# Modulation weights in two halves with longer rows, the first two u weight tiles in one transfer, and x transposed by a diagonal

## The chip, the cores and the metric

The kernel runs on one core of one Trainium2 chip. The metric is device microseconds of one execution; the figure of a version is the median of its runs.

In this text PE is TensorE (the matmul engine), PEld its weight loads, DVE VectorE, ACT ScalarE, POOL GpSimd and SP the engine that issues most transfers. Every engine works through its own queue in order; a transfer that SP can't issue yet holds up all that are queued behind it on SP.

## What is computed

One layer of a streaming encoder, over 1024 prompt rows and 32 sample rows of width 1024. What matters here is its beginning:

```python
mod = silu(c) @ w_mod + b_mod                     # c: one row for the prompt, one for the samples
shift, scale, gate = split(mod, 3)                # 1024 columns each
h = x / sqrt(mean(x*x) + eps) * g_norm            # each row of x
h = h * (1 + scale) + shift
z = h @ w_in                                      # 5704 columns, the first 512 are u
u, zs, q, k, v, ... = split(z)
```

Behind it come the state space model on u, an indexed sparse attention, gates, an output projection and a last normalization; they are the same before and after the change.

## The kernel before, in words

`h` is wanted with its columns on the partitions (`hH` and `hL`, the high and low parts of each value), since it is the moving operand of every projection. The 1056 rows are cut into three blocks of 256, 384 and 416 columns of `h` (`BW`), made of 2, 3 and 4 row tiles (`ROWS`; the last tile holds the 32 sample rows). The 1024 columns of x are eight column tiles, k = 0 to 7.

The opening goes through these steps; the two letters are those of the list `START` (lines 48 to 59), which fixes the order of the work on all engines by hand. Its tokens are read from left to right (lines 771 to 782) and each engine gets its instructions in that order.

- `sq`, `ss`, `sc` (lines 211 to 223): ScalarE sums the squares of a row tile, DVE and POOL make the row's reciprocal root `rstd`, and DVE multiplies the whole 128 x 1024 tile by it, in place.
- `ld` (line 739): SP issues loads. `ld21` of the modulation weights loads column group 2, half 1; `ldx67` loads row tiles 6 and 7; `ldz` the next projection weights and the SSM's loads. What stands ahead of the list (lines 749 to 759) is issued at once.
- `mm`, `row`, `co`, `ap` (lines 284 to 304): modulation in four column groups j of 256 columns, each with scale columns (h = 0) and shift columns (h = 1). One group and half is a tile of 8 x 256 columns from a transfer with rows of 1 KB (line 282). TensorE makes eight f32 products with 32 columns of weights, four side by side in the array; ScalarE copies the result to SBUF; two products with a selection matrix (`sel2`) turn it so that it lies on the partitions; three small DVE steps give `scl` and `sh` for column tiles 2j and 2j+1.
- `xt` (line 227): TensorE transposes column tile k of all row tiles of a block into PSUM, by an identity. There are two such PSUM buffers.
- `hf`, `sp` (lines 233 and 241): ScalarE applies `scl` and `sh`; DVE splits the result into `hH` and `hL`.
- `wl` (line 729): the u weights of a group of 128 columns are split into high and low parts; group 0 by ScalarE and DVE, group 1 on POOL. They are loaded in two transfers with rows of 512 bytes (lines 726 and 250).
- `ub` (line 543): three products (lines 271 to 273) add column tile k of a block to u of group 0 or 1.
- `a` with a number: so many of the small DVE steps of the SSM's constants.

Tiles of the tag `wm` share five buffers (`WB`): modulation weights, and row tiles 6 to 8 of x. A load into a reused buffer waits on SP until the last reader is through.

After the list, line 526 turns the SSM's C matrices by transposes (line 529), and the projections for the rest of z run through `Stream`, interleaved with the SSM and the attention by fixed costs.

Of the kernel before, what the change touches and what calls it, by code (L numbers as in the profile page):

```python
# [7 lines left out]
F32 = mybir.dt.float32  # L8
# [4 lines left out]
ALU = mybir.AluOpType  # L13
# [3 lines left out]
T, TS, D = 1024, 32, 1024  # L17
# [4 lines left out]
KT = 8  # L22
# [8 lines left out]
WB = 5  # L31
# [14 lines left out]
MR, ML, YS, YW, HI, HG, JO, SF = (), 1, 10, 15, 0, 0, 8, (2, 2, 2, 1)  # L46
C_U, C_ZS, C_Q, C_K, C_V, C_ZA, C_QI, C_KI, C_GM = 0, 512, 1024, 1536, 2048, 2560, 3072, 3584, 3656
START = """
    sq0 ss0 sq1 sc0 ss1 sq2 sc1 ss2 sc2 mm00 srow ldw21 a13 xt00 row00 xt01 co00 mm01 ldw30 row01 wl00 co01
    ap0 mm10 ldw31 a2 hf00 row10 xt02 sp00 hf01 co10 sp01 xt03 mm11 ldx67 a6 wl10 ub000 row11 co11 sq3 ub100  # L50
    ap1 ub001 a1 ub101 hf02 ss3 a1 hf03 sp02 sq4 sp03 ub002 ub102 sq5 ss4 ub003 sc3 ub103 sc4 mm20 ldx8 ldz
    ss5 row20 a2 co20 sc5 a5 mm21 xt10 row21 xt11 hf10 co21 hf11 ap2 xt12 sp10 xt13 hf12 mm30 hf13 xt04 sp11
    row30 ub010 hf04 co30 sp12 xt05 xt14 hf05 ub110 sp13 hf14 mm31 sp04 xt15 row31 xt06 hf15 ub011 sp05 co31
    sq6 xt07 ap3 ub111 ub012 sp14 hf06 ub112 hf07 xt16 sp15 ub013 sq7 xt17 sp06 ub113 up hf16 ub004 sp07
    ub104 hf17 ub014 sp16 sq8 ub114 sp17 ub005 zs ub105 ss6 ub015 ss7 ss8 ub115 ub006 ub106 sc6 ub016 ub116
    sc7 ub007 sc8 ub107 ue00 ub017 ue10 a5 xt20 ue01 xt21 ub117 hf20 ue11 sp20 hf21 xt22 a1 ub020 hf22 xt23
    sp21 ub120 hf23 xt24 sp22 ub021 ub121 hf24 sp23 xt25 ub022 hf25 sp24 xt26 ub122 hf26 ub023 sp25 xt27
    ub123 sp26 hf27 ub024 ub124 sp27 ub025 ub125 ub026 ub126 ub027 ub127 ue02 ue12
    """
# [1 line left out]
GROW = [[n for g_, _, n in ROWS if g_ == g] for g in range(3)]  # L61


def body(nc, tc, I, O, dbg=None):
# [3 lines left out]
    te, ve, se, ge, sp = nc.tensor, nc.vector, nc.scalar, nc.gpsimd, nc.sync  # L68
# [48 lines left out]
    idf = cst.tile([128, 128], F32, name="idf")  # L117
# [6 lines left out]
    w_in = I["w_in"].rearrange("o d e -> (o d) e")  # L124
    w_mod = I["w_mod"].rearrange("o d e -> (o d) e")
# [31 lines left out]
    sc2 = cst.tile([128, 2, 8], F32)  # L157
# [3 lines left out]
    scP = cst.tile([128, 8, 32], F32, name="scP")  # L161
# [7 lines left out]
    bmod = pcol[:, 8:32]  # L169
# [5 lines left out]
    srow = pp.tile([80, 128], F32)  # L175
# [12 lines left out]
    scl = cst.tile([128, 8, 2], F32)  # L188
# [7 lines left out]
    def xload(i):  # L196
        g, r, n = ROWS[i]
        if i < 2:
            xt = stg.tile([128, D], F32, name="xt", tag="stg")
        elif i < 5:  # L200
            xt = XH[i // 4][:, D * (i == 3):D * (i == 3) + D]
        elif i == 5:
            xt = pa.tile([128, D], F32, name="xt", bufs=1)
        else:
            if i % 2 == 0:
                XW.append(pa.tile([128, 2, D], F32, name="xw", tag="wm", bufs=WB))
            xt = XW[-1][:, i % 2]
# [10 lines left out]
        ve.tensor_scalar(ss[:n, i:i + 1], ss[:n, i:i + 1], 1.0 / D, EPS, op0=ALU.mult, op1=ALU.add)  # L218
        ge.tensor_tensor(rstd[:n, i:i + 1], ss[:n, i:i + 1], nhalf[:n, i:i + 1], op=ALU.pow)

    def xscale(i):
        g, r, n = ROWS[i]
        ve.tensor_scalar_mul(XG[g][r][:n], XG[g][r][:n], rstd[:n, i:i + 1])

    PX, HX = {}, {}

    def xtrans(g, k):
        px = ps_z("px")
        PX[g, k] = px
        for r, n in enumerate(GROW[g]):  # L230
            te.transpose(px[:, r * 128:r * 128 + n], XG[g][r][:n, k * 128:(k + 1) * 128], idf[:n, :n])
# [16 lines left out]
    def wload(src, kt, n, pool=None):  # L248
        raw = (pool or wst).tile([128, kt, n], F32, tag="raw", name="raw", bufs=2)
        sp.dma_start(raw, src.rearrange("(k p) e -> p k e", p=128))  # L250
        return raw
# [21 lines left out]
        te.matmul(ps, wl, xh, start=False, stop=last)  # L273
# [5 lines left out]
    def mod_load(j, h):
        wm = WM[j, h] = pa.tile([128, 8, 256], F32, name="wm", tag="wm", bufs=WB)  # L280
        c = (1024, 0)[h] + 256 * j
        sp.dma_start(wm, w_mod[:, c:c + 256].rearrange("(k p) e -> p k e", p=128))

    def mod_mm(j, h):
        for k in range(8):
            te.matmul(pmrow[32 * (k % 4):32 * (k % 4) + 32, 256 * h:256 * h + 256], scP[:, k], WM[j, h][:, k],
                      start=k < 4, stop=k >= 4)

    def mod_row(j, h):
        MR_[j, h] = pa.tile([128, 256], F32, name="mrow", bufs=2)  # L290
        se.copy(MR_[j, h], pmrow[:, 256 * h:256 * h + 256])

    def mod_cols(j, h):
        for i in range(2):
            ch = (8, 0)[h] + 2 * j + i
            te.matmul(pmod[:, 2 * ch:2 * ch + 2], MR_[j, h][:, 128 * i:128 * i + 128], sel2, start=True, stop=True)

    def mod_apply(j):
        kk = slice(2 * j, 2 * j + 2)
        ks = slice(8 + 2 * j, 10 + 2 * j)  # L300
        bc2 = lambda ap: ap.unsqueeze(2).to_broadcast([128, 2, 2])
        ve.tensor_tensor(scl[:, kk], pm[:, ks], bc2(bmod[:, ks]), op=ALU.add)
        ve.tensor_tensor(scl[:, kk], scl[:, kk], bc2(gcol[:, kk]), op=ALU.mult)
        ve.tensor_tensor(sh[:, kk], pm[:, kk], bc2(bmod[:, kk]), op=ALU.add)
# [166 lines left out]
    for k in range(7):  # L471
        n = 1 << k
# [250 lines left out]
    ord_.enter_context(tc.manual_schedule())  # L723
    raw = {}

    def uload(q):
        raw[q] = wload(w_in[:, C_U + 128 * q:C_U + 128 * q + 128], KT, 128)

    def uparts(q):
        UW[q] = wparts(raw[q], KT, 128, leng=ve) if q == 0 else wparts(raw[q], KT, 128, pool=pa, heng=ge, bufs=1)  # L730
# [20 lines left out]
    mod_load(0, 0)
    mod_load(0, 1)
    uload(0)
    mod_load(1, 0)
    mod_load(1, 1)
    uload(1)
    for i in range(3, 6):
        xload(i)
    mod_load(2, 0)
    ve.tensor_add(sel2, idf[:, 0:2], idf[:, 32:34])  # L760
    for j in (64, 96):
        ve.tensor_add(sel2, sel2, idf[:, j:j + 2])
# [1186 lines left out]
```

## Time and profile before

| | us |
|---|---|
| median of three runs | 1014.81 |
| lowest and highest of them | 1013.17, 1015.25 |
| the profiled execution | 1013.51 |
| its span, first to last instruction | 1011.5 |
| first u product starts | 24.70 |
| last u product of the list starts | 70.37 |
| first transpose after the list starts | 70.56 |

| engine, busy over the span | us | share |
|---|---|---|
| PE | 968.2 | 96% |
| DVE | 763.3 | 75% |
| ACT | 524.6 | 52% |
| POOL | 234.6 | 23% |

How to read it. A row of the timeline has the start, the time of the merged instructions, the engine and line, the operation, its output and inputs, their shapes and how many instructions stand in it; in brackets the idle time before it and what ended that. Matmuls are pipelined, so that the time of one overlaps the next, and what one costs is seen from start to start. A row of the stages has, for each engine, the busy time and the number of instructions, then the TensorE clock that was granted (1.00 is full speed), the busy share of the 16 DMA engines and GB/s.

### The profile page before, as it was taken

Reading aid. Unit: us, or ns where it says so; the run is one execution under the profiler, and the core shown is the slowest. Engines: PE = TensorE matmul, PEld = TensorE weight load, DVE = VectorE, ACT = ScalarE, POOL = GpSimd, SP = SyncE. Lnnn points to the kernel's source line nnn. Section 1 sums busy time; section 2 is a strip of 40 time slices with the busy share of each in tenths; the row PEclk is TensorE's granted clock in tenths of the full one; section 3 lists DMA queues with packets and bytes.
Section 4 is the critical chain, followed back from the end, with each engine's and each line's share of the span. In section 5 each row is a group of like instructions: output and inputs, shape, how many; then the busy total and the mean of one; then the engine's idle time right before and its main releaser. Section 6 shows DMA issues by size and latency. Waiting matters only on the chain.

```text
span 1011.5 us, 16910 instructions
## 1 busy us (share of the span) xinstructions
PE 968.2 (96%) x6034; PEld 904.1 (89%) x6034; DVE 763.3 (75%) x1747; ACT 524.6 (52%) x1126; POOL 234.6 (23%) x443
## 2 busy tenths in 40 slices
PE   5999999999999999999999989999998999999997
PEld 2789999999998898999999979899897989898786
DVE  4669979994776878889999976577577785885543
ACT  3642234433555656858896365565575564443111
POOL 3202400000000024343322743233222222430000
PEclk9999999999999999999999999999999999999999
DMA  9923425437484222333323422231329403552311
GB/s 315 289 66 101 133 70 140 113 95 203 164 256 151 64 63 64 105 83 98 118 74 114 141 87 64 85 106 55 107 66 332 136 22 109 182 188 105 126 63 62
DMA packets 134400, 124.24 MB, mean 123 GB/s; under 512 B 20401, under 2 KB 115077, under 8 KB 134317
## 3 DMA queue, kind: packets, MB, share of 16 engines
q1 hardware_dynamic: 133376, 122.62, 39.3%
q8 instruction: 47, 0.77, 0.3%
q10 hardware_dynamic: 780, 0.52, 0.2%
q14 instruction: 37, 0.30, 0.1%
q0 software_dynamic: 160, 0.03, 0.0%
HBM read 87.74 MB, written 34.83 MB: 121 GB/s over the span
## 4 chain that ended last, share of the span: by engine, by line
PE 50%; DVE 14%; ACT 10%; issue 4%; DMA 1%; POOL 0%; SPq 0%; POOLq 0%; ACTq 0%; DVEq 0%
PE pz L271 8%; PE pz L272 7%; PE pz L273 7%; ACT junkb L1567 7%; PE pss L1403 3%; PE pt L1496 3%; DVE junk L1569 3%; PE psm L1918 3%; PE psm L1919 3%; PE psm L1920 3%; PE pspo L1515 2%; PE pspo L1513 2%; PE psm L272 1%; PE psm L273 1%; PE psm L271 1%
## 5 line engine op out<-in xcount | busy, mean ns | idle before, releaser
L271 PE MATMUL pz<-hH,wh 128*128 128x384 f32 (+4 forms) x744 | 254.5, 342 | 2.4 <-ACT tg L713 2.0
L272 PE MATMUL pz<-hL,wh 128*128 128x384 f32 (+4 forms) x744 | 246.2, 331 | 0.0
L273 PE MATMUL pz<-hH,wl 128*128 128x384 f32 (+4 forms) x744 | 246.0, 331 | 0.0
L264 POOL TENSOR_TENSOR wl<-raw,wh 128x256 fp32r<-128x256 f32 (+1 forms) x180 | 134.7, 776 | 126.5 <-ACT wh L259 116.0
L271 PEld LDWEIGHTS pz<-hH,wh 128*128 128x128 f32 (+1 forms) x744 | 140.4, 189 | 7.5 <-ACT tg L713 2.3
L272 PEld LDWEIGHTS pz<-hL,wh 128*128 128x128 f32 (+1 forms) x744 | 139.9, 188 | 1.8
L273 PEld LDWEIGHTS pz<-hH,wl 128*128 128x128 f32 (+1 forms) x744 | 139.6, 188 | 1.4
L1567 ACT ACTIVATE junkb<-sco,thr 128x768 bf16<-128x768 f32 (+3 forms) x128 | 96.7, 756 | 31.0 <-DVE thr L1643 20.1
L1569 DVE TENSOR_SCALAR_CACHE_REDUCE junk<-sco,thr 128x1024 bf16<-128x1024 f32 (+2 forms) x96 | 105.5, 1098 | 2.2
L271 PE MATMUL pss<-hH,wh 128*128 128x256 f32 (+2 forms) x304 | 97.6, 321 | 0.1
L272 PE MATMUL pss<-hL,wh 128*128 128x256 f32 (+2 forms) x304 | 95.7, 315 | 0.0
L273 PE MATMUL pss<-hH,wl 128*128 128x256 f32 (+2 forms) x304 | 95.4, 314 | 0.0
L263 POOL CAST wh<-raw 128x256 fp32r<-128x256 f32 x88 | 38.0, 471 | 180.9 <-PE pz L272 109.6
L1498 ACT CAST PH<-pt 128x512 fp32r<-128x512 f32 (+2 forms) x96 | 43.0, 482 | 41.5 <-PE pt L1496 37.4
L1499 DVE TENSOR_TENSOR PL<-pt,PH 128x512 fp32r<-128x512 f32 (+2 forms) x96 | 50.4, 551 | 14.6 <-ACT PH L1498 13.7
L271 PEld LDWEIGHTS pss<-hH,wh 128*128 128x128 f32 x304 | 58.6, 193 | 2.6 <-issue 1.6
L272 PEld LDWEIGHTS pss<-hL,wh 128*128 128x128 f32 x304 | 58.1, 191 | 0.3 <-DVE hL L78 0.2
L1236 DVE SCALAR_TENSOR_TENSOR sco<-rl,wi,sco 128x384 f32<-128x384 f32 (+6 forms) x49 | 46.9, 963 | 15.2 <-ACT rl L1231 14.1
L273 PEld LDWEIGHTS pss<-hH,wl 128*128 128x128 f32 x304 | 58.1, 191 | 0.0
L1231 ACT ACTIVATE rl<-pss 128x384 f32<-128x384 f32 (+6 forms) x56 | 40.9, 738 | 28.6 <-PE pss L1229 23.1
L1416 ACT ACTIVATE Sm<-Sm,mx 128x128 f32<-128x128 f32 (+8 forms) x68 | 52.7, 775 | 0.8 <-DVE mx L1409 0.8
L1920 PE MATMUL psm<-o,mL 128*128 128x512 f32 (+1 forms) x136 | 51.8, 381 | 0.0
(401 smaller groups left out, 2174.9 us busy)
## 6 DMA issues: line engine op xcount, KB each, us to landing
raw<-in_w_in SPq DMA_DIRECT2D x44, 512.0 KB
thD<-tg SPq DMA_DIRECT2D x16, 528.0 KB
wm<-in_w_mod SPq DMA_DIRECT2D x8, 1024.0 KB
tgl<-thD SPq DMA_DIRECT2D x8, 528.0 KB
m<-thD SPq DMA_DIRECT2D x8, 528.0 KB
rraw<-in_w_mod SPq DMA_DIRECT2D x4, 1024.0 KB
kd<-kd SPq DMA_DIRECT2D x32, 128.0 KB
xo<-in_x_prompt SPq DMA_DIRECT2D x8, 512.0 KB
```

Source lines behind the costliest of these rows:

```text
L264: leng.tensor_sub(wl[:, c], raw[:, c], f32(wh[:, c]))
L271: te.matmul(ps, wh, xh, start=first, stop=False)
L272: te.matmul(ps, wh, xl, start=False, stop=False)
L273: te.matmul(ps, wl, xh, start=False, stop=last)
L1231: se.activation(rl[:m, :nk].rearrange("p (b c) -> p b c", c=w_), pv, AF.Relu)
L1236: ve.scalar_tensor_tensor(sco[i][:m, :nk], rl[:m, :nk], w, sco[i][:m, :nk], op0=ALU.mult, op1=ALU.add)
L1416: se.activation(P, P, AF.Exp, scale=-1.0, bias=self.mx, accum_out=self.rs)
L1498: se.copy(PH[:, b0:b1_, oc], src)
L1499: ve.tensor_sub(PL[:, b0:b1_, oc], src, f32(PH[:, b0:b1_, oc]))
L1567: se.activation(junkb[:m, :nk], x[:m], AF.Sign, bias=t, accum_out=cnt[:m, k:k + 1])
L1569: ve.tensor_scalar(junk[:m, :nk], x[:m], t, None, op0=ALU.is_lt, op1=ALU.add, accum_out=cnt[:m, k:k + 1])
L1920: te.matmul(ps, ml, wh, start=False, stop=last)
```

## The change

- Modulation is computed in two halves of 512 scale and 512 shift columns (column tiles 0 to 3, then 4 to 7). A half comes in four pieces of 256 rows of w_mod; each piece is two transfers with rows of 2 KB. A piece is multiplied by four f32 products of 512 columns, side by side in the array; the results of four pieces are summed in one PSUM bank. One copy, four products with `sel4` and three DVE steps finish a half.
- The two u weight tiles are loaded in one transfer with rows of 1 KB, into a buffer of the tag `wm`.
- x isn't scaled any more. Instead DVE makes for each row tile a 128 x 128 diagonal matrix of its `rstd` (`dg`), and the transpose becomes a product of the raw x tile with this diagonal. For block 0 one `xt` makes two column tiles in one PSUM buffer.
- Row tiles 5 and 6, and 7 and 8, share buffers of the tag `wm`; row tile 5 has no buffer of its own any more.
- The order of the loads and the list `START` are new: x0, x1, the first half, u, x2 to x4, the second half, x5 to x8, the rest. The end of the list, from `sp21` on, is as before.

```diff
 START = """
-    sq0 ss0 sq1 sc0 ss1 sq2 sc1 ss2 sc2 mm00 srow ldw21 a13 xt00 row00 xt01 co00 mm01 ldw30 row01 wl00 co01
-    ap0 mm10 ldw31 a2 hf00 row10 xt02 sp00 hf01 co10 sp01 xt03 mm11 ldx67 a6 wl10 ub000 row11 co11 sq3 ub100
...
+    sq0 ss0 sq1 dg0 ss1 dg1 mm00 srow ldw10 a13 xt00 mm01 ldw11 xt02 mm02 ldw12 mm03 ldw13 row0 co0 ap0
+    hf00 sp00 hf01 wl00 wl10 ldx56 ub000 sp01 ub001 hf02 sp02 sq2 ss2 hf03 sp03 ub100 ub002 ub101 ub003 ub102 ub103
+    sq3 ss3 sq4 ss4 dg2 dg3 dg4 a8 xt10 hf10 sp10 xt11 hf11 sp11 mm10 ldx78 ldz ub010 ub110 xt12 hf12 sp12 ub011 ub111
+    xt13 hf13 sp13 mm11 ub012 ub112 a8 ub013 ub113 mm12 xt04 a10 xt06 mm13 row1 co1 ap1 hf04 sp04 hf05 sp05 ub004 ub104
+    xt14 hf06 sp06 ub005 ub105 sq5 ss5 hf07 sp07 ub006 ub106 xt15 hf14 sp14 dg5 ub007 ub107 sq6 ss6 hf15 sp15 ub014
+    ub114 xt16 sq7 ss7 hf16 sp16 dg6 ub015 ub115 xt17 sq8 ss8 hf17 sp17 dg7 dg8 ub016 ub116 up ub017 ub117 zs ue00 ue10
+    xt20 ue01 xt21 hf20 ue11 sp20 hf21 xt22 a1 ub020 hf22 xt23
...
-    def xscale(i):
+    DG = {}
+
+    def xdiag(i):
         g, r, n = ROWS[i]
-        ve.tensor_scalar_mul(XG[g][r][:n], XG[g][r][:n], rstd[:n, i:i + 1])
+        DG[g, r] = pa.tile([128, 128], F32, name="dg", bufs=5)
+        ve.tensor_scalar_mul(DG[g, r][:n, :n], idf[:n, :n], rstd[:n, i:i + 1])
...
     def xtrans(g, k):
-        px = ps_z("px")
-        PX[g, k] = px
-        for r, n in enumerate(GROW[g]):
-            te.transpose(px[:, r * 128:r * 128 + n], XG[g][r][:n, k * 128:(k + 1) * 128], idf[:n, :n])
+        pb = ps_z("px")
+        for j in range(2 if g == 0 else 1):
+            px = PX[g, k + j] = pb[:, 256 * j:]
+            for r, n in enumerate(GROW[g]):
+                te.matmul(px[:, r * 128:r * 128 + n], XG[g][r][:n, (k + j) * 128:(k + j + 1) * 128], DG[g, r][:n, :n],
+                          start=True, stop=True)
...
+    def mod_load(h, i):
+        wm = WM[h, i] = pa.tile([128, 2, 2, 512], F32, name="wm", tag="wm", bufs=WB)
+        for k in range(2):
+            sp.dma_start(wm[:, k], w_mod[256 * i + 128 * k:256 * i + 128 * k + 128, 0:2048]
+                         .rearrange("p (c a e) -> p c a e", c=2, a=2)[:, :, h])
+
+    def mod_mm(h, i):
+        for k in range(2):
+            for c in range(2):
+                o = 32 * (2 * k + c)
+                te.matmul(pmrow[o:o + 32, :], scP[:, 2 * i + k], WM[h, i][:, k, c], start=i == 0, stop=i == 3)
+
+    def mod_row(h):
+        MR_[h] = pa.tile([128, 512], F32, name="mrow", bufs=1)
+        se.copy(MR_[h], pmrow)
+
+    def mod_cols(h):
+        for i in range(4):
+            k = 4 * h + i
+            te.matmul(pmod[:, 4 * k:4 * k + 4], MR_[h][:, 128 * i:128 * i + 128], sel4, start=True, stop=True)
...
-    def uload(q):
-        raw[q] = wload(w_in[:, C_U + 128 * q:C_U + 128 * q + 128], KT, 128)
+    def uload():
+        t = pa.tile([128, KT, 256], F32, name="wm", tag="wm", bufs=WB)
+        sp.dma_start(t, w_in[:, C_U:C_U + 256].rearrange("(k p) e -> p k e", p=128))
+        for q in range(2):
+            raw[q] = t[:, :, 128 * q:128 * q + 128]
...
-    for i in range(3):
+    xload(0)
+    xload(1)
+    for i in range(4):
+        mod_load(0, i)
+    uload()
+    for i in range(2, 5):
         xload(i)
```

More of the change, by code (lines that the diff above doesn't have):

```diff
@@ L48 @@
 START = """
-    sq0 ss0 sq1 sc0 ss1 sq2 sc1 ss2 sc2 mm00 srow ldw21 a13 xt00 row00 xt01 co00 mm01 ldw30 row01 wl00 co01
-    ap0 mm10 ldw31 a2 hf00 row10 xt02 sp00 hf01 co10 sp01 xt03 mm11 ldx67 a6 wl10 ub000 row11 co11 sq3 ub100
[L51 to L56, printed above, removed]
+    sq0 ss0 sq1 dg0 ss1 dg1 mm00 srow ldw10 a13 xt00 mm01 ldw11 xt02 mm02 ldw12 mm03 ldw13 row0 co0 ap0
[5 more added lines that the diff above has]
+    xt20 ue01 xt21 hf20 ue11 sp20 hf21 xt22 a1 ub020 hf22 xt23
     sp21 ub120 hf23 xt24 sp22 ub021 ub121 hf24 sp23 xt25 ub022 hf25 sp24 xt26 ub122 hf26 ub023 sp25 xt27
@@ L201, in xload @@
             xt = XH[i // 4][:, D * (i == 3):D * (i == 3) + D]
-        elif i == 5:
-            xt = pa.tile([128, D], F32, name="xt", bufs=1)
         else:
-            if i % 2 == 0:
+            if i % 2 == 1:
                 XW.append(pa.tile([128, 2, D], F32, name="xw", tag="wm", bufs=WB))
-            xt = XW[-1][:, i % 2]
+            xt = XW[-1][:, 1 - i % 2]
         load_rows(xt, g, r, n, sp)
@@ L273, in mm3 @@
         te.matmul(ps, wl, xh, start=False, stop=last)
-    sel2 = pa.tile([128, 2], F32, name="sel2", bufs=1)
+    sel4 = pa.tile([128, 4], F32, name="sel4", bufs=1)
     WM, MR_ = {}, {}
[L279 to L302, printed above, removed]
+    def mod_load(h, i):
[3 more added lines that the diff above has]
+                         .rearrange("p (c a e) -> p c a e", c=2, a=2)[:, :, h])
@@ L303, in mod_apply @@
+    def mod_apply(h):
+        kk = slice(4 * h, 4 * h + 4)
+        ks = slice(8 + 4 * h, 12 + 4 * h)
+        bc2 = lambda ap: ap.unsqueeze(2).to_broadcast([128, 4, 2])
+        ve.tensor_tensor(scl[:, kk], pm[:, kk, 1], bc2(bmod[:, ks]), op=ALU.add)
         ve.tensor_tensor(scl[:, kk], scl[:, kk], bc2(gcol[:, kk]), op=ALU.mult)
-        ve.tensor_tensor(sh[:, kk], pm[:, kk], bc2(bmod[:, kk]), op=ALU.add)
+        ve.tensor_tensor(sh[:, kk], pm[:, kk, 0], bc2(bmod[:, kk]), op=ALU.add)
     scol = cst.tile([128, 5, 16], F32)
@@ L747, in load @@
             f()
-    for i in range(3):
-        xload(i)
[L751 to L762, printed above, removed]
+    xload(0)
[4 more added lines that the diff above has]
+    for i in range(2, 5):
+        xload(i)
+    for c in range(2):
+        ve.tensor_add(sel4[:, 2 * c:2 * c + 2], idf[:, 32 * c:32 * c + 2], idf[:, 64 + 32 * c:66 + 32 * c])
     ve.memset(dl, 0.0)
     pmod, pmrow = ps_t("pmod"), ps_t("pmrow")
-    pm = pmod[:, 0:32].rearrange("p (k s) -> p k s", s=2)
-    STEP = dict(sq=xsquare, ss=xrstd, sc=xscale, mm=mod_mm, row=mod_row, co=mod_cols, ap=mod_apply, xt=xtrans,
+    pm = pmod[:, 0:32].rearrange("p (k c s) -> p k c s", c=2, s=2)
+    STEP = dict(sq=xsquare, ss=xrstd, dg=xdiag, mm=mod_mm, row=mod_row, co=mod_cols, ap=mod_apply, xt=xtrans,
                 hf=xmod, sp=xsplit, wl=lambda q, _: uparts(q), ub=ublock, srow=srows, zs=lambda: Z.split(0), up=utiles,
@@ L780, in body @@
             STEP[n](*(int(c) for c in t[len(n):]))
-        if t == "wl00":
+        if t == "mm00":
             ssm_shifts()
```

## The prediction

> **What bounds the kernel now.** I read the page first, then the busy time by stage, then TensorE's timeline of the opening, then who waits for whom. The diff touches only the opening: until the SSM input u is projected for its first two column groups. That opening ends where the first transpose of line 529 starts, at 70.56 us.
>
> ```profile
> span 1011.5 us, 16910 instructions
> PE 968.2 (96%) x6034; PEld 904.1 (89%) x6034; DVE 763.3 (75%) x1747; ACT 524.6 (52%) x1126; POOL 234.6 (23%) x443
> ```
> ```profile
> 11.14:24.70 13.56, 12.45 (x85) 6.61 (x85) 7.24 (x32) 3.09 (x6) 0.93 (x2) 1.00 1.11 342
> 24.70:48.50 23.80, 22.38 (x168) 17.86 (x165) 14.30 (x48) 14.71 (x29) 5.75 (x12) 0.93 1.06 310
> 48.50:70.56 22.06, 22.06 (x131) 19.53 (x130) 13.95 (x35) 11.16 (x24) 2.22 (x4) 1.00 0.17 27
> 70.56:1011.50 940.94, 910.71 (x5656) 859.76 (x5654) 723.62 (x1618) 490.65 (x1059) 219.51 (x407) 0.99 0.37 115
> ```
> ```profile
> 11.14 1.93 PE L286 MATMUL pmrow<-wm,scP 128*32 128x256 f32 x16 [3.73 <-DMA wm<-in_w_mod]
> ...
> 24.70 0.58 PE L271 MATMUL pss<-hH,wh 128*128 128x256 f32 x1
> ...
> 30.27 0.41 PE L271 MATMUL pss<-hH,wh 128*128 128x256 f32 x1
> 30.49 0.41 PE L272 MATMUL pss<-hL,wh 128*128 128x256 f32 x1
> ...
> 46.80 0.49 PE L231 MATMUL px<-idf,xh 128*128 128x128 f32 x3
> 47.05 0.42 PE L271 MATMUL pss<-hH,wh 128*128 128x384 f32 x1
> 47.31 0.34 PE L272 MATMUL pss<-hL,wh 128*128 128x384 f32 x1
> 47.49 0.34 PE L273 MATMUL pss<-hH,wl 128*128 128x384 f32 x1
> ...
> 48.53 0.28 PE L271 MATMUL pss<-hH,wh 128*128 128x256 f32 x1
> 48.65 0.29 PE L272 MATMUL pss<-hL,wh 128*128 128x256 f32 x1
> ...
> 59.83 0.27 PE L231 MATMUL px<-idf,xt 128*128 128x128 f32 x1
> 59.94 0.55 PE L231 MATMUL px<-idf,xw 128*128 128x128 f32 x3
> 60.42 0.46 PE L271 MATMUL pss<-hH,wh 128*128 128x416 f32 x1
> 60.72 0.35 PE L272 MATMUL pss<-hL,wh 128*128 128x416 f32 x1
> 60.91 0.35 PE L273 MATMUL pss<-hH,wl 128*128 128x416 f32 x1
> ...
> 70.56 0.60 PE L529 MATMUL pt<-idf,cld 128*128 128x128 f32 x4
> ```
> ```profile
> DVE dsk L534 <- PE pt L533: 4.8, 1, 4.8
> ```
> In the stage rows (columns: stretch and length, busy us and count of PE, weight loads, DVE, ACT and POOL, granted clock, DMA share, GB/s) the loads run at their limit until 48.5 us, and TensorE is busy in nearly all of it too. From 48.5 to 70.56 DMA is at 0.17 and TensorE at 22.06 of 22.06: what ends the opening is TensorE's own list, not the last byte. At its end DVE has waited 4.8 us for TensorE, so all engines begin the rest, where TensorE is busy 910.71 of 940.94 us, on TensorE's word. I therefore carry a shift of the opening's end through to the end at one to one.
>
> Matmuls are pipelined, so what one costs is the distance to the next start: 0.12 us at 256 columns (48.53 to 48.65), 0.18 at 384 (47.31 to 47.49; 0.175 over many), 0.19 at 416. The same 256-column product took 0.21 to 0.22 us at 30.27: TensorE then ran at half pace. Two rows show that pace change:
>
> ```profile
> 31.00:34.40 3.40, 2.11 (x24) 1.21 (x23) 2.24 (x10) 0.37 (x1) 0.55 (x1) 1.00 1.09 348
> 34.41:37.82 3.41, 3.38 (x24) 2.11 (x24) 0.00 (x0) 0.94 (x2) 0.00 (x0) 0.50 1.09 347
> ```
> A stretch of 3.4 us with 2.11 us busy is followed by a stretch at clock 0.50; that one, busy for 3.38, is followed by full pace. (The 1.00 that the views give before 31.0 is no measurement; the distances say half.)
>
> Account of before, from the first u product at 24.70 to 70.56: 48 triples of u products, 16 for each block, are 48 x (0.118 + 0.175 + 0.19) = 23.2 us. 64 transposes are left by then. A transpose costs 0.11: three start at 46.80, the next product at 47.05, and that one is 0.08 longer than its neighbour. The set with 32 sample rows takes 59.83 to 60.42 and makes the next product 0.11 longer, 0.70 for four, so the short one costs 0.37. 56 x 0.109 + 8 x 0.37 = 9.1. Four modulation products are 4 x 1.0 = 4.0 and six column turns of four instructions 2.7. Together 39.0; the other 6.9 us are half pace (about 3.1 until 31.0 and 1.7 from 34.4) and waits (2.1).
>
> **The change part by part.**
>
> ```profile
> 16.00:20.00 4.00, 2.89 (x24) 1.53 (x20) 2.02 (x8) 1.54 (x3) 0.00 (x0) 1.00 1.09 348
> 24.00:26.00 2.00, 2.00 (x14) 1.30 (x7) 0.00 (x0) 1.10 (x2) 1.84 (x5) 1.00 1.05 412
> ...
> 334.00:336.00 2.00, 2.00 (x12) 1.99 (x12) 1.97 (x4) 1.36 (x2) 0.00 (x0) 1.00 1.01 389
> ```
> *Loads.* While 1 KB rows of w_mod flow the core reads 348 GB/s; with 4 KB rows of x 412; in a stretch with 2 KB rows (the gate columns of the same w_mod) 389. A 1.05 MB piece of modulation weights so costs 2.70 us and not 3.01: 2.5 us less for eight. Both u tiles in 1 KB rows cost 3.0; they had 512-byte rows, for which I take some 1 us more. All in all the loads end 3.5 us sooner. The first modulation product moves from 11.14 to about 9.5 (one x tile less ahead, 1.3, and 0.3 of the piece), the fourth piece of the first half lands at 9.5 + 3 x 2.7 = 17.6, u at 20.6, the last piece of the second half at about 35.
>
> On SP's queue the second half's four pieces wait for buffers that the first half's products release, and x5 to x8, the next weights and the SSM loads are queued behind them. The last release is at about 20; the transfers queued by then last until 23.4, so I cost these waits at nothing. Without that cover a piece could come up to 2.7 us late, against the 6 us by which TensorE reaches it later than it lands (below).
>
> *First u product.*
>
> ```profile
> 11.59 0.22 DVE L184 COPY srow<-ldt 16x128 f32<-16x128 f32 x1
> ...
> 18.17 1.22 DVE L264 TENSOR_TENSOR wl<-raw,wh 128x1024 fp32r<-128x1024 f32 x1 [1.91 <-ACT wh L259]
> ...
> 20.70 0.42 DVE L78 TENSOR_TENSOR hL<-hf,hH 128x256 fp32r<-128x256 f32 x1
> ```
> ```profile
> 17.09 1.05 ACT L259 CAST wh<-raw 128x1024 fp32r<-128x1024 f32 x1
> 19.77 0.56 ACT L237 ACTIVATE hf<-px,sh,scl 128x256 f32<-128x256 f32 x1 [1.63 <-DVE sh L304]
> ```
> The first half needs all four pieces before any scale is known. TensorE stands behind the small transpose that needs the copy at 11.59, then has four diagonal transposes, a modulation product, four more, and two products: at half pace about 1.7 us each, to 20.7; if full pace comes at about 17, to 19.1. Then in a row: the copy of 512 columns (about half of the 1.05 of 1024: 0.55), 8 column turns (0.9 to 1.7), the three small DVE steps (0.4), two scalings (1.1), the cast (1.05), the subtraction (1.22) and handovers: 25.2 us, or 27.4 at half pace throughout; 24.4 if full pace comes at 14. I take 25.2, because 12 to 20.7 is as dense as the stretch at 34.41, after which full pace came.
>
> *Transposes.* A product of a raw x block with a diagonal is a plain f32 matmul, which TensorE runs as two instructions:
>
> ```profile
> 137.55 2.07 PE L909 MATMUL pss<-Uq,Bc 128*128 128x133 f32 x16
> 139.37 0.42 PE L271 MATMUL pz<-hH,wh 128*128 128x384 f32 x1
> ```
> Eight f32 products are 16 instructions here, in 1.82 us: 0.114 each, 0.228 a product against 0.109 for a transpose. Of the 64 left at the first u product, 56 x 0.228 + 8 x 0.48 = 16.6, in place of 9.1: plus 7.5 us on the engine that ends the stage.
>
> *Row scaling.*
>
> ```profile
> L223 DVE TENSOR_SCALAR xw<-xw,rstd 128x1024 f32<-128x1024 f32 (+1 forms) x3 | 2.3, 751 | 0.7 <-POOL rstd L219 0.6
> ```
> Nine steps of 0.75 on DVE go; nine diagonals of 128 columns come, between 0.17 (the smallest DVE steps of this opening) and 0.42 (the 256-column subtraction); I take 0.2. Some 5 us leave DVE, which is busy 14.30 of 23.80 and 13.95 of 22.06 us while TensorE is busy throughout: no gain. The column sums that follow the rows' squares (ScalarE, POOL) stay as they are. The start list also issues 40 instead of 36 of the small SSM steps within the opening, 0.8 us less for DVE afterwards; worth nothing while TensorE sets the pace.
>
> *Modulation products and turns.*
>
> ```profile
> 44.61 0.50 PE L296 MATMUL pmod<-sel,mrow 128*128 128x2 f32 x4
> ```
> ```profile
> 317.45 1.06 PE L1173 MATMUL pg<-rraw,scP 128*32 128x512 f32 x8
> ```
> The new form, four products of 512 columns side by side, is that of line 1173: 1.06, like the old one at full pace. After the first u product stand four of them (4.0, as before) and one set of eight turns (0.9) for six sets of four (2.7): minus 1.8.
>
> *New waits.* After the last product of the second half nothing is queued that TensorE could do: copy to SBUF (0.9 with its handovers), then, after the turns, DVE's three steps (0.4), a scaling (0.56), a cast and a subtraction (0.3 and 0.42) and handovers, 1.9. The last block starts with 0.6 until its first rows are split. Together 3.4, where before had 2.1.
>
> *Half pace.* TensorE idles from about 21 to 25.2, so the products after it start at half pace, for one to two stretches of 3.4 us: 1.2 to 2.9 us lost; the 2.8 us of waiting at about 43 may bring another stretch, 1.1 to 1.7. I take 2.4 of 0 to 4.6, before lost 4.8.
>
> Sum: 25.2 + 23.2 + 16.6 + 4.0 + 0.9 + 3.4 + 2.4 = 75.7, against 70.56: plus 5.1. By difference: first product +0.5, transposes +7.5, turns -1.8, waits +1.3, half pace -2.4. The profiled execution took 1013.51 us (span 1011.5 and 2.0 around it), so 1018.6; it lies 1.3 under the median of the runs, 1014.81, which makes 1019.9.
>
> **The rivals.**
>
> *The loads decide* (faster). If the opening ended a fixed time after the last weights, it would move by the 3.5 us that the loads gain: 1011.3. For it: DMA above 1.06 until 48.5 and weights awaited at 11.14. Against it: 22 us of TensorE alone after the loads. It decides only if TensorE has done the first half of both blocks when the last piece lands at 35; I have it there at about 42.
>
> *Only the last block's transposes count* (no change). If TensorE still waits 4 us or more for data between 25 and 45, the doubling is hidden there and the 32 transposes of the last block remain, 3.8 us, against 3.5 of earlier loads: 1015.1. For it: the 2.1 us of waits and the half pace before. Against it: blocks 0 and 1 have their u weights by 20.6 and nothing missing but TensorE's time.
>
> *One instruction after all* (faster). If the diagonal product ran as one instruction of 0.114, 0.3 instead of 7.5 would be added: 1012.7. Line 909 and the x4 of line 296 for two products speak against it.
>
> *The pace follows plain products only* (slower, by less).
>
> ```profile
> 34.44 1.93 PE L286 MATMUL pmrow<-wm,scP 128*32 128x256 f32 x16 [0.84 <-DMA wm<-in_w_mod]
> 36.31 1.54 PE L231 MATMUL px<-idf,xh 128*128 128x128 f32 x6
> ```
> If transposes did not count for the granted clock, making them products would bring full pace by 14 and again one stretch after 25: 24.4 + 44.7 + 3.4 + 1.2 = 73.7, plus 3.1, 1017.9. The stretch at 34.41 held one modulation product and six transposes; the product alone would fill 57%, less than the 62% of the stretch before it, after which the pace fell, and yet full pace followed. So transposes do seem to count. The Trainium skill's page "TensorE: Matmul & The Clock Gate", section "Part 4: PE-mode transpose", states the contrary: that transposes don't count as busy for the clock. By that rule this rival is the forecast; the two rows just read disagree with it.
>
> *Half pace throughout* (slower, by more). If the wide f32 products don't bring full pace at all before the u products do: 27.4 + 44.7 + 3.4 + 3.0 = 78.5, plus 8, 1022.8. For it: before stayed at half pace until 31.0 with TensorE busy 12.45 of 13.56.
>
> **How the numbers follow.** Forecast 0.38, pace by plain products 0.20, half pace throughout 0.12: slower 0.70. Only the last block: 0.14 no change. Loads decide 0.12 and one instruction 0.04: faster 0.16. A measurement of this kernel can tell about 0.2%, 2 us, from no change. The likeliest time is 1019.9. The range runs from 1014.0, which takes in the case of no change, to 1023.0, the end of the longest half pace; what it leaves out is the faster cases.
>
> **What would show it.** In the profile after: px products as twice as many instructions, 0.11 apart; the modulation rows at 389 GB/s; the first u product at 24 to 27 us; TensorE without data waits from there except ahead of the second half's first product; the last modulation weights landed some 6 us before their product starts; line 529 at 74 to 78 us. Wrong would be: line 529 at 71 or sooner, transposes 0.06 apart, or a rest of the kernel that is not 941 us long.

## The result and the profile after

| | before, us | after, us |
|---|---|---|
| median of four runs each | 1014.65 | 1022.00 |
| lowest and highest | 1013.17, 1015.25 | 1021.55, 1023.14 |
| the profiled execution, its span | 1013.51, 1011.5 | 1021.77, 1020.0 |
| first u product | 24.70 | 23.15 |
| end of the opening (first transpose of the SSM's C matrices) | 70.56 | 78.46 |
| the rest, to the end of the span | 940.94 | 941.54 |

The ratio of after to before is 1.0079, with a 95% interval of 1.0063 to 1.0095. The changed kernel is 0.8% slower, and nearly all of it is in the opening: 7.9 us there, 0.6 in the remaining 941.

The busy time by engine on the page of after. TensorE has 4.9 us more, DVE 2.5 less than before:

```profile
PE 973.1 (95%) x6026; PEld 907.5 (89%) x6026; DVE 760.8 (75%) x1740; ACT 522.8 (51%) x1120; POOL 237.8 (23%) x443
```

The stages of after, cut at its first modulation product, its first u product, the first u product that needs the second half, and the end of the opening. The columns are those of the stage rows of before:

```profile
8.15:23.15 15.00, 10.94 (x57) 4.07 (x57) 5.13 (x24) 2.59 (x5) 3.63 (x7) 0.95 1.05 386
23.15:46.18 23.03, 19.97 (x129) 15.01 (x129) 13.90 (x52) 8.31 (x16) 4.78 (x8) 0.87 1.03 316
46.18:78.46 32.28, 32.05 (x184) 29.79 (x185) 16.25 (x42) 17.60 (x36) 2.32 (x7) 0.91 0.11 18
78.46:1020.00 941.54, 909.55 (x5656) 858.25 (x5654) 723.92 (x1614) 490.40 (x1059) 222.58 (x407) 0.99 0.38 115
```

The loads are over early, as planned: the last stage has DMA at 0.11. But that stage is 32 us of nothing but TensorE, where before had 22. Before, TensorE was busy 12.45 of 13.56 us ahead of its first u product and 22.38 of 23.80 in the stage behind it. Now it idles 4 us in the first stage and 3 in the second, and the granted clock is below 1 in all three.

TensorE's timeline of after, at the two places where it pauses, and at the end:

```profile
8.15 3.22 PE L291 MATMUL pmrow<-wm,scP 128*32 128x512 f32 x8 [0.77 <-DVE pcol L166]
...
11.43 1.10 PE L232 MATMUL px<-dg,xt 128*128 128x128 f32 x8
...
17.62 1.05 PE L291 MATMUL pmrow<-wm,scP 128*32 128x512 f32 x4 [0.33 <-DMA wm<-in_w_mod]
19.36 1.05 PE L300 MATMUL pmod<-sel,mrow 128*128 128x4 f32 x8 [0.69 <-ACT mrow L295]
23.15 0.58 PE L273 MATMUL pss<-hH,wh 128*128 128x256 f32 x1 [2.74 <-ACT wh L261]
...
24.63 0.58 PE L275 MATMUL pss<-hH,wl 128*128 128x256 f32 x1 [0.68 <-DVE wl L266]
25.36 0.58 PE L273 MATMUL pss<-hH,wh 128*128 128x256 f32 x1 [0.15 <-DVE hH L76]
...
29.48 1.50 PE L232 MATMUL px<-dg,xh 128*128 128x128 f32 x12
...
39.85 2.05 PE L232 MATMUL px<-dg,xt 128*128 128x128 f32 x16
41.83 1.07 PE L291 MATMUL pmrow<-wm,scP 128*32 128x512 f32 x8
43.60 1.06 PE L300 MATMUL pmod<-sel,mrow 128*128 128x4 f32 x8 [0.70 <-ACT mrow L295]
46.18 0.58 PE L273 MATMUL pss<-hH,wh 128*128 128x256 f32 x1 [1.52 <-DVE hH L76]
...
78.46 0.60 PE L533 MATMUL pt<-idf,cld 128*128 128x128 f32 x4
```

At the opening's end DVE waits for TensorE, as it did before:

```profile
DVE dsk L538 <- PE pt L537: 4.9, 1, 4.9
```

Read three things in the timeline. Four diagonal products are eight instructions (11.43, x8). The brackets name what each pause ends with: a copy or cast of ScalarE, then a step of DVE, no DMA behind 17.62. And at 41.83 the last modulation product starts with no bracket at all, right behind the diagonal products at 39.85: its weights had landed, TensorE came to it late.

The same opening, cut at the steps of the granted clock:

```profile
14.74:18.15 3.41, 2.78 (x16) 0.43 (x12) 0.00 (x0) 0.00 (x0) 0.00 (x0) 1.00 1.06 370
18.15:21.57 3.42, 1.58 (x12) 0.97 (x8) 0.62 (x3) 1.01 (x2) 0.87 (x2) 1.00 1.07 385
21.57:24.98 3.41, 1.15 (x3) 0.79 (x3) 2.64 (x4) 3.41 (x8) 3.25 (x5) 0.50 1.03 398
24.98:28.39 3.41, 3.25 (x13) 2.78 (x13) 3.00 (x10) 2.26 (x5) 2.41 (x5) 0.50 1.04 385
28.39:31.81 3.42, 3.42 (x31) 2.56 (x29) 2.60 (x12) 1.34 (x2) 0.62 (x2) 1.00 1.06 391
...
42.05:45.46 3.41, 1.90 (x16) 0.97 (x8) 0.41 (x3) 0.81 (x2) 0.00 (x0) 1.00 0.84 111
45.46:48.87 3.41, 2.69 (x11) 2.52 (x12) 2.64 (x9) 2.75 (x6) 0.55 (x1) 0.50 0.50 71
48.87:52.29 3.42, 3.42 (x18) 3.42 (x17) 1.30 (x5) 1.71 (x3) 0.55 (x1) 0.50 0.28 54
```

Each stretch with a pause (1.58 and 1.90 us busy of 3.41) is followed by one at clock 0.50, which lasts two stretches both times. So two pauses, two spells of half pace.

### The profile page after: what moved, and what is told of

Same layout as the page of the kernel before. It is cut to its first block, busy times and chain, and to the rows that moved or that the text cites. A ratio compares the mean times of both kernels' runs of the same rounds, so it can differ in the third digit from the quotient of the medians.

```text
span 1020.0 us, 16892 instructions
## 1 busy us (share of the span) xinstructions
PE 973.1 (95%) x6026; PEld 907.5 (89%) x6026; DVE 760.8 (75%) x1740; ACT 522.8 (51%) x1120; POOL 237.8 (23%) x443
```

## The experiments

All ratios are to the kernel before, run on the same chip as the experiment; the median of the kernel before lay between 1012.6 and 1013.5 us on them. Openings are those of the profiled executions. The theory is the forecast's: the doubled transposes cost 7.5 us on TensorE's path, and the other changes come close to cancelling each other. Its rivals are those of the prediction.

**The diagonals undone.** The change as it is, but DVE scales the rows again and TensorE transposes:

```diff
-        DG[g, r] = pa.tile([128, 128], F32, name="dg", bufs=5)
-        ve.tensor_scalar_mul(DG[g, r][:n, :n], idf[:n, :n], rstd[:n, i:i + 1])
+        ve.tensor_scalar_mul(XG[g][r][:n], XG[g][r][:n], rstd[:n, i:i + 1])
...
-                te.matmul(px[:, r * 128:r * 128 + n], XG[g][r][:n, (k + j) * 128:(k + j + 1) * 128], DG[g, r][:n, :n],
-                          start=True, stop=True)
+                te.transpose(px[:, r * 128:r * 128 + n], XG[g][r][:n, (k + j) * 128:(k + j + 1) * 128], idf[:n, :n])
```

> The changed kernel with rows scaled by DVE and plain transposes again; loads, halves and order stay as changed. Theory A (a diagonal product is two instructions, 0.117 us more than a transpose for each of the 64 that follow the first u product, all on TensorE's path): the opening ends 7.5 us sooner than 78.5, at about 71, and the time is about 1014.5. Rival B (the doubling is mostly hidden, the halves with their two pauses are what costs): at most 3 us less, about 1019. Rival C (only plain products count for the granted clock, transposes don't): the first full pace comes after the first u products and not at 11, the first u product starts at 25 or later, and the gain is 4 to 5 us, about 1017.5.

Measured: ratio 1.0022 [1.0009, 1.0035]; the end of the opening in its timeline:

```profile
73.25 0.60 PE L531 MATMUL pt<-idf,cld 128*128 128x128 f32 x4
```

The diagonals are 5.2 of the 7.9 us, and most of the slowdown: more than the 3 us of rival B, less than the 7.5 of the theory. Rival C's course wasn't seen: the first u product started at 23.10, and full pace was there early without diagonals (the four transposes at 11.24 took 0.53 us to the next start, those of before, at half pace, 0.85 at 13.19). The spell of half pace behind the first pause lasted three stretches here instead of two. But without the diagonals the change is still a little slower than before, although its loads end sooner.

**The diagonals alone, in the order of before.** The same edit the other way round, made in the kernel before. To make room, five diagonals lie in a free part of an x buffer, and `hf` has three buffers instead of four.

```diff
-        ve.tensor_scalar_mul(XG[g][r][:n], XG[g][r][:n], rstd[:n, i:i + 1])
+        DG[g, r] = XH[1][:, 1024 + 128 * i:1152 + 128 * i] if i < 5 else pa.tile([128, 128], F32, name="dg", bufs=4)
+        ve.tensor_scalar_mul(DG[g, r][:n, :n], idf[:n, :n], rstd[:n, i:i + 1])
...
-            te.transpose(px[:, r * 128:r * 128 + n], XG[g][r][:n, k * 128:(k + 1) * 128], idf[:n, :n])
+            te.matmul(px[:, r * 128:r * 128 + n], XG[g][r][:n, k * 128:(k + 1) * 128], DG[g, r][:n, :n],
+                      start=True, stop=True)
```

> The kernel before with the diagonal products alone (its loads, column groups and order kept; one buffer of hf less, to make room for the diagonals). A: 64 x 0.117 = 7.5 us more, the opening ends at about 78, the time is about 1022. B: before's waits and half pace hide most of it, plus 2 to 4 us, 1017 to 1019. C: full pace comes one or two stretches of 3.4 us before 31, which gives back 2 to 3 us, about 1019.5.

Measured: ratio 1.0072 [1.0046, 1.0098], opening 78.46 (the same figure as after's, by another way). Here the diagonals cost 7.9 us in all. That figure is a mixture, for the pace changed too: full pace was there by 15.38 (the modulation product there took 1.07 us) and not only from 31.0, though it fell twice again, while TensorE waited 1.22 us for DVE at 27.34 and 1.62 for weights at 31.55. The price is clean behind the last modulation product, from where both kernels run at full pace. First the kernel before, then this one:

```profile
42.47 1.07 PE L286 MATMUL pmrow<-wm,scP 128*32 128x256 f32 x16
```
```profile
45.15 1.07 PE L290 MATMUL pmrow<-wm,scP 128*32 128x256 f32 x16
```

From there to the opening's end it is 28.09 against 33.31 us, 5.2 more, and doubling the 45 transposes that follow makes 5.3 (37 x 0.119 + 8 x 0.11). So there the doubling has the price forecast. In the order of the change a part of it is hidden; which part, the last two experiments show.

**Work in the second pause, plain products and transposes.** Idle products whose result nobody reads stand in the pause around the second half's turns: ten products (`w3`, `w7`), or twenty transposes (`w6`, `w14`) of the same length in all.

```diff
-    xt13 hf13 sp13 mm11 ub012 ub112 a8 ub013 ub113 mm12 xt04 a10 xt06 mm13 row1 co1 ap1 hf04 ...
+    xt13 hf13 sp13 mm11 ub012 ub112 a8 ub013 ub113 mm12 xt04 a10 xt06 mm13 row1 w3 co1 w7 ap1 hf04 ...
```

> The changed kernel with ten products of the identity with itself, whose results nobody reads, put where TensorE waits around the turns of the second half (three ahead of them, seven behind). A: the stretch at half pace from 45.5 to 52.3 goes, the opening ends 3 us sooner at about 75.5, the time is about 1019. B: the pause itself is what costs; nothing gained, up to 0.5 us lost, 1022 to 1022.5.

> The same pause filled with twenty transposes of the identity (six and fourteen) in place of ten products, so that TensorE is busy equally long. A (transposes count for the granted clock like products): full pace stays, about 1019, like the filling with products. C (they don't count): the pace falls at about 45 as in the changed kernel, about 1022.

Measured: 1.0101 [1.0076, 1.0126] and 1.0100 [1.0071, 1.0129], openings 79.40 and 78.90. The expectation on the clock was met, that on the time was missed. Two lines of the transposes' timeline and two rows of its stretches:

```profile
45.92 1.73 PE L555 MATMUL pmod<-idf 128*128 128x128 f32 x14
49.17 0.38 PE L273 MATMUL pss<-hH,wh 128*128 128x256 f32 x1 [1.52 <-DVE hH L76]
```
```profile
45.14:48.55 3.41, 2.51 (x22) 2.27 (x22) 0.41 (x3) 0.32 (x1) 0.00 (x0) 1.00 0.53 75
48.55:51.97 3.42, 2.72 (x21) 2.53 (x22) 2.75 (x10) 3.36 (x8) 0.55 (x1) 1.00 0.25 51
```

In the first row 1.73 of the 2.51 us are transposes; without them 0.78 would be left, less than the 1.90 after which the pace fell in after. It stays at 1.00, as with plain products (2.53 us busy there). So these transposes do count for keeping full pace. The time was lost elsewhere: the fill writes `pmod`, the PSUM tile that DVE's `ap` steps read, so DVE waited until the last idle product was through, and the way from the last modulation product to the first of the new u products grew by 1.6 us (43.24 to 49.17, against 41.83 to 46.18); and the first spell of half pace lasted three stretches instead of two in both runs, which made the product of line 291 late (43.24 in this timeline against 41.83). The fill had to go elsewhere.

**Work in both pauses, written where nobody reads.** The same idea with `pmrow` as target (tokens `v`), in both pauses, once with diagonals and once with scaled rows and plain transposes:

```diff
-    ... mm03 ldw13 row0 co0 ap0 hf00 sp00 hf01 wl00 wl10 ldx56 ub000 sp01 ub001 ...
+    ... mm03 ldw13 row0 w3 co0 v18 ap0 hf00 sp00 hf01 wl00 wl10 ldx56 ub000 v4 sp01 ub001 ...
-    ... mm13 row1 co1 ap1 hf04 ...
+    ... mm13 row1 w3 co1 v8 ap1 hf04 ...
```

> The changed kernel with both pauses filled by idle products (identity by identity, results unread): three ahead of the turns of a half, then eighteen and four around the first u product, eight ahead of the second half's first; unlike the first filling they write a PSUM bank that DVE's scale steps don't read, so that these don't wait for them. A (pace): no stretch at half pace from 21 to 28 or 31 nor from 45 to 52; against the changed kernel 1.5 to 3 us from the first pause and 2.6 from the second, opening at 73 to 74.5, time about 1017.5. B (the pauses themselves): 1022 as changed.

> The same filling with rows scaled by DVE and plain transposes: loads and halves as changed, diagonals undone, both pauses filled. A: 5.5 to 6 us less than the version with plain transposes alone (two stretches of half pace, 10.2 and 6.8 us long, give back 3 and 2.6), opening at 67.5 to 68, time 3 us under before. B: as the version with plain transposes alone, 0.2% above before.

Measured: 1.0061 [1.0041, 1.0081] with diagonals, opening 75.99; 1.0003 [0.9991, 1.0015] with plain transposes, opening 70.45. Both gained less than expected (openings of 73 to 74.5 and 67.5 to 68). The stages of the first, cut at the same events as after's, now stand at clock 1.00; ahead of about 13.7 us that figure is no measurement, for eight diagonal instructions at 11.91 took 1.89 us, which is half pace:

```profile
8.66:24.70 16.04, 15.73 (x99) 9.54 (x100) 6.30 (x24) 3.76 (x6) 4.73 (x8) 1.00 1.05 388
24.70:46.40 21.70, 21.62 (x161) 17.02 (x160) 12.77 (x52) 7.26 (x15) 3.71 (x6) 1.00 1.03 312
46.40:75.99 29.59, 29.37 (x188) 27.11 (x187) 16.07 (x42) 17.46 (x35) 2.32 (x7) 1.00 0.10 17
```

The last stage is 29.59 us long instead of 32.28: 2.7 us of half pace gone from it. The first u product comes 1.55 us later with the fill (0.4 of it because the last piece of the first half landed later in this execution, 18.03 against 17.62), yet block 1's transposes start at 29.27 instead of 29.48: what half pace costs in the first pause is covered by TensorE's early start, since the operands come late anyway. By these two openings half pace is worth 78.46 - 75.99 = 2.5 us in sum. And the distance between the two kernels, both at full pace, is 5.5 us: again the diagonals' price in this order.

**The same fill in the kernel before.** If half pace is what can be won, before has some too.

```diff
-    sq0 ss0 sq1 sc0 ss1 sq2 sc1 ss2 sc2 mm00 srow ... row01 wl00 co01
+    sq0 ss0 sq1 sc0 ss1 sq2 sc1 ss2 sc2 w8 mm00 srow ... row01 wl00 w4 co01
...
-    ss5 row20 a2 co20 sc5 a5 mm21 ...
+    ss5 row20 w2 a2 co20 sc5 w3 a5 mm21 ...
```

> The kernel before with idle products in its waits: eight ahead of the first modulation product, four and two and three at later turns. A (half pace also costs before 4.8 us until 38): full pace from about 14 instead of 31, up to 4 us less, 1010 to 1011.5, if the waits left over don't bring half pace back. B: before was bound by its loads until 40, so nothing is gained, 1013 to 1014.5.

Measured: 0.9987 [0.9974, 1.0000], opening 69.37. The gain, 1.3 us by a ratio whose interval ends at no change, is a fraction of the 3 to 4 that were hoped for. Its timeline has a pause for weights, and its stretches then stay at half pace for 10 us, however busy:

```profile
18.81 1.07 PE L286 MATMUL pmrow<-wm,scP 128*32 128x256 f32 x16 [2.29 <-DMA wm<-in_w_mod]
```
```profile
20.45:23.86 3.41, 3.41 (x23) 1.81 (x23) 1.67 (x8) 0.40 (x1) 0.24 (x1) 0.50 1.14 341
23.86:27.28 3.42, 3.42 (x16) 3.40 (x16) 1.64 (x7) 2.55 (x6) 3.18 (x7) 0.50 1.02 386
27.28:30.69 3.41, 3.33 (x14) 2.71 (x12) 2.90 (x7) 2.29 (x4) 2.64 (x4) 0.50 1.09 349
```

**The loads with short rows.** Each transfer of modulation weights of the change is cut into two, so that its rows are 1 KB as before:

```diff
-            sp.dma_start(wm[:, k], w_mod[256 * i + 128 * k:256 * i + 128 * k + 128, 0:2048]
-                         .rearrange("p (c a e) -> p c a e", c=2, a=2)[:, :, h])
+            for b in range(2):
+                sp.dma_start(wm[:, k, :, 256 * b:256 * b + 256], w_mod[256 * i + 128 * k:256 * i + 128 * k + 128, 0:2048]
+                             .rearrange("p (c a e) -> p c a e", c=2, a=2)[:, :, h, 256 * b:256 * b + 256])
```

> The changed kernel with its modulation weights in rows of 1 KB (each transfer cut in two of 256 columns). A (TensorE's list ends the opening; only the first half's last piece is awaited): the first half lands 1.3 us later, the first u product at 24.4, the second half's delay is not seen, plus 1.3, 1023.3. Rival L (the loads decide): plus 2.6 or more, 1024.6. If rows make no difference: 1022.

Measured: 1.0088 [1.0064, 1.0112], not to be told from the change itself (1.0079). The first stage of its profile, to its first u product:

```profile
8.15:24.90 16.75, 11.84 (x58) 4.81 (x58) 4.98 (x23) 2.93 (x7) 3.71 (x7) 0.97 1.08 363
```
The loads are slower (363 against 386 GB/s) and the first product comes 1.75 us later; the opening of this execution ends 2.1 later, at 80.56. So in the profiles what the first half's last piece is late goes through to the end. But this execution was the slowest of its four, and by the ratios the whole differs by 0.9 us with an uncertainty of about 3: the runs don't say whether the longer rows gain the 1.3 us expected, more, or nothing.

**Useful work in the second pause.** Four triples of block 1's u products are held back until behind the second half's last modulation product, so that the pause holds work that has to be done anyway, and four idle products remain in it; with diagonals and with plain transposes:

```diff
-    xt13 hf13 sp13 mm11 ub012 ub112 a8 ub013 ub113 mm12 xt04 a10 xt06 mm13 row1 w3 co1 v8 ap1 hf04 ...
+    xt13 hf13 sp13 mm11 a8 mm12 xt04 a10 xt06 mm13 row1 ub012 ub112 co1 ub013 ub113 v4 ap1 hf04 ...
```

> Kernel with the change and both pauses filled as before, but the second pause now holds work that has to be done anyway: four triples of block 1's u products (column tiles 2 and 3) are held back, two triples while ScalarE copies the second half's result, two triples and four idle products behind the turns. If the waits are the mis-sized term of the sum and are made by the order alone, the second half's last product starts 2.1 us sooner (at about 39.9; its weights landed by then), the first product of the second half's column tiles follows 1.8 to 2.1 us sooner than with idle products, the opening ends at 74.0 (75.99 with idle products) and the whole is 0.20% shorter than that version: ratio 1.004. Rival, that the second half waits for its weights or for ScalarE and DVE in any order: the last product starts no sooner than 41.5, the opening ends at 75.5 to 76.5, ratio 1.006.

> The same order with scaled rows and plain transposes (all else of the change kept). If the waits are made by the order alone, the opening ends at 68.5 (70.46 with idle products in the second pause), ratio 0.998, so faster than both kernels by 0.2% and more. If DVE, which scales rows again, holds the column tiles of the second half back, 70.0 to 70.5 and ratio 1.000. Beside the version with diagonals in the same order the distance is again 5.5 us if what a transpose costs has nothing to do with the second pause.

Measured: 1.0029 [1.0015, 1.0043] with diagonals; 0.9983 [0.9970, 0.9995] with plain transposes, the only version whose interval lies below that of no change, if only by 0.17%. The last modulation product, the first product of the second half's column tiles and the end of the opening, with diagonals and then plain:

```profile
39.32 1.06 PE L291 MATMUL pmrow<-wm,scP 128*32 128x512 f32 x8
...
44.23 0.36 PE L273 MATMUL pss<-hH,wh 128*128 128x256 f32 x1
...
73.67 0.60 PE L533 MATMUL pt<-idf,cld 128*128 128x128 f32 x4
```
```profile
29.86 0.33 PE L231 MATMUL px<-idf,xh 128*128 128x128 f32 x1 [0.67 <-DVE xh L222]
30.68 0.66 PE L231 MATMUL px<-idf,xh 128*128 128x128 f32 x4 [0.49 <-DVE xh L222]
...
43.66 0.36 PE L271 MATMUL pss<-hH,wh 128*128 128x256 f32 x1
...
68.48 0.60 PE L531 MATMUL pt<-idf,cld 128*128 128x128 f32 x4
```

The product and both openings came within 0.6 us of what was expected; the weights had landed by 39.32, and what TensorE lost in the second pause was lost by the order alone. The two kernels differ by 5.19 us, and the rows say where. From the first product of the second half to the end it is 29.44 against 24.82 us: 4.6 of the 5.2 that the doubling of the 44 transposes behind that point makes (36 x 0.119 + 8 x 0.11). Ahead of it, 20 transposes doubled make 2.4, of which 0.6 are left. There the plain version pays for something else: its transposes at 29.86 and 30.68 wait for DVE's row scaling (line 222). A stretch and a line of DVE of the plain version:

```profile
24.00:28.00 4.00, 3.92 (x31) 3.48 (x30) 3.90 (x11) 3.27 (x7) 3.00 (x5) 1.00 1.05 384
```
```profile
29.05 1.58 DVE L222 TENSOR_SCALAR xh<-xh,rstd 128x1024 f32<-128x1024 f32 x2 [0.45 <-POOL rstd L216]
```

Until 28 us DVE (the third figure) has hardly a gap, with diagonals as without: 3.90 of 4.00 us in both. So in neither version does DVE come to block 1's rows sooner, and from there a scaled tile takes it 0.75 us, a diagonal 0.28.

These runs part the 7.9 us step by step, each from two profiles: the order and the loads with both pauses filled and plain transposes, -2.1 (70.56 to 68.48); the second pause left to idle products, +2.0 (to 70.45); half pace after both pauses, +2.8 (to 73.25); the diagonals, +5.2 (to 78.46). By the ratios the steps are -1.7, +2.0, +1.9 and +5.8 us, each with an uncertainty of about 2. So the loads and the order, with the pauses filled, are worth about 2 us, and the pauses cost more than that.

## Why the prediction was right, and where it was not

The sign and the main cause held: TensorE's own list sets the end, and the product with a diagonal is two instructions. The predicted 1019.9 is 2.1 below the median, because the opening ended at 78.46 and not at 75.7; that alone would be 2.8, but the forecast also added 1.3 us from the profiled execution to the median, of which 0.2 were there. Two signs that the forecast named were missed narrowly: the first u product came before 24 us and the opening's end after 78. Point by point:

- *What bounds the kernel.* Held. The rest took 941.54 us, and DVE waited 4.9 us for TensorE at the opening's end, as before.
- *The work.* 23.2 + 16.6 + 4.0 + 0.9 = 44.7 us behind the first u product held in its parts, at full pace: 16 instructions of the diagonal products take 1.98 us from 39.85 to the next start, 0.12 each, a modulation product 1.0, the turns 1.06 from their first start to their last end (19.36, 43.60).
- *First u product, 25.2.* It came at 23.15, but that was too simple a mark. The forecast had DVE's subtraction ahead of it; in fact only the third product of the triple needs it, and that started at 24.63. With the pause filled the first came at 24.70. The forecast had full pace from about 17 and TensorE's own list in front, until 19.1; in fact full pace was there from 11.4 (the modulation product at 12.45 took 1.06 us), and TensorE waited for the last piece, which came at 17.62, as forecast. The chain behind it took 6.0 us, 6.1 in the forecast.
- *New waits, 3.4.* This is the step that failed. In the version with both pauses filled, which has no half pace behind its first u product, 24.70 + 44.7 = 69.4, and the opening ended at 75.99: 6.6 us of waits. From 24.70 to 29.27 eight triples (2.8) took 4.6; here the forecast had nothing. In after the brackets at 24.63 and 25.36 name DVE there, and DVE was busy 3.90 of the 4.00 us from 24 to 28 in the last two experiments, with two casts of 0.8 us among it (last section). The second pause took 2.6 beside its product and turns, where 2.8 was forecast, so that part held. Block 1 and the modulation products in between, 29.27 to 41.93, lost 0.9, and all behind the second pause 1.4, where 0.6 was forecast. (Up to 0.8 in the first figure may be the idle products themselves.) That the second pause is lost time the last two experiments show: with work in it the opening ended 2.3 and 2.0 us sooner.
- *Half pace, 2.4.* It was 2.5, and the agreement is in part luck. The pace fell where it was said, once after each pause, but the forecast put 1.2 to 2.9 us of the loss behind the first pause and 1.1 to 1.7 behind the second; in fact nearly all of it lies behind the second, 2.7, for behind the first the operands were late as well.
- *Row scaling, no gain.* In the new order it gains some 2 us. The forecast looked at DVE's share of a stage, and there DVE had room. But in the plain version of the last experiment DVE is full until 28 us, and the scaling of block 1's rows stands directly ahead of their transposes. The two waits in the rows are 1.2 us, two more behind them (0.16 at 32.49 and 0.15 at 33.08, for DVE's splits) 0.3, and 1.8 of the 2.4 are gone; the other 0.3 aren't assigned. The 7.9 us of the old order can't be compared term by term, since the pace differed there too. In the forecast's sum this gain has no term of its own: without the diagonals the waits would have been larger still.

The rivals. *The loads decide* fell: the last weights had landed by the time TensorE came to them, with either length of rows. *Only the last block's transposes count* was half right: the doubling is in fact mostly hidden between 25 and 44 us, but behind that point 44 transposes remain, not 32, and what loads and order gain was lost in the pauses. *One instruction after all* fell with the x8 at 11.43. *The pace follows plain products only* fell for keeping full pace: twenty transposes in the second pause kept it at 1.00 just as ten products did. The page "TensorE: Matmul & The Clock Gate" of the Trainium skill, section "Part 4: PE-mode transpose", says otherwise, for bf16 transposes; for the f32 transposes of this case the runs decide against it, as far as keeping the pace goes. For regaining it they leave the rival open: with the diagonals alone in the old order full pace was there by 15.38 and not from 31.0, as the rival has it, while the stretch of before from 34.41, with six transposes, was followed by full pace. *Half pace throughout* gave 1022.8, close to the result, but not by its mechanism: full pace was there from 11.4 to 21.57 and from 28.39 to 45.46.

## What to carry to other kernels

A product with a diagonal instead of a transpose takes work from DVE and doubles it on TensorE for f32, so look at which of the two ends the stage, and look at it at the tile where they meet, not by the stage's average. When fewer, larger steps replace many small ones, count the chain of every other engine that now has to run once in a row while the main engine has nothing to do, and move work that has to be done anyway into that gap before you think of anything else. Idle work that only keeps the clock up must write where nobody reads.

## What the runs showed of the hardware

The granted clock changes in steps of 3.41 us (21.57 to 28.39 and 45.46 to 52.29 in after are two each), and how busy TensorE was in the stretch before goes with it, though not without exception. After 2.51 us busy of 3.41 full pace stayed; after 2.11 (before), 1.90 and 1.58 (after) it fell. In the old order with diagonals it fell at 18.40 after 2.07, but stayed after 2.05; three stretches of that run:

```profile
14.99:18.40 3.41, 2.07 (x25) 1.31 (x24) 1.58 (x8) 1.32 (x2) 0.00 (x0) 1.00 1.10 345
...
25.22:28.64 3.42, 2.05 (x15) 1.56 (x13) 3.19 (x9) 2.78 (x7) 3.23 (x6) 1.00 1.05 370
28.64:32.05 3.41, 1.71 (x19) 1.13 (x22) 2.15 (x13) 1.10 (x2) 1.42 (x3) 1.00 1.10 347
```

So the busy share alone isn't the whole rule; what else counts isn't shown. No whole stretch has to be idle: the second pause of after idles 0.70 and 1.52 us around the turns. The Trainium skill's page "TensorE: Matmul & The Clock Gate", section "Part 1: The HAM clock gate (the "warmup" mystery)", names in its table at least one idle window of about 3.4 us as the condition for the slow state, and further on a kernel whose short idles between groups of products made the clock swing; here less than a whole window was enough. The way back isn't a matter of the busy time alone either: after 3.25 us at half pace it rose (24.98 to 28.39 in after), after 2.69 it didn't. In the kernel before with fill not even 3.42 sufficed, so that the spell lasted three stretches, while that of before from 34.41 lasted one; what decides was not found.

DVE's cast of a 128 x 256 block took 0.81 us twice in after and 0.28 to 0.29 in the other casts of that size:

```profile
24.50 0.81 DVE L76 CAST hH<-hf 128x256 fp32r<-128x256 f32 x1
...
25.77 0.81 DVE L76 CAST hH<-hf 128x256 fp32r<-128x256 f32 x1
...
27.02 0.28 DVE L76 CAST hH<-hf 128x256 fp32r<-128x256 f32 x1
27.80 0.28 DVE L223 TENSOR_SCALAR dg<-idf,rstd 128x128 f32<-128x128 f32 x1
```

POOL splits the second u weight tile at the same time; two of its subtractions:

```profile
23.57 1.59 POOL L266 TENSOR_TENSOR wl<-wm,wh 128x256 fp32r<-128x256 f32 x1
...
25.64 0.79 POOL L266 TENSOR_TENSOR wl<-wm,wh 128x256 fp32r<-128x256 f32 x1
```

The slow casts end at 25.31 and 26.58, some 0.15 us after these two subtractions (25.16 and 26.43), and the first subtraction, twice as long as its neighbour, overlaps DVE's own long subtraction of the first weight tile. So each seems to stand still while the other works. The Trainium skill's page "SBUF — State Buffer", section "SBUF: two separate sides", says that DVE and GpSimd share a pair of ports under an exclusive lock, for DVE's steps in a 2-port mode or with two inputs. The times agree with such a lock, but no trace shows whether a cast, which has one input, runs in that mode, and no run took POOL's work away, so the cause isn't shown. The diagonal itself took 0.28 us where 0.2 was forecast, to no effect.
